# Layer 0's three products per weight tile: 272 + 272 + 272 columns become 288 + 256 + 272

## The chip, the core and the metric

One core of a Trainium2 chip runs the whole program. The time is the device time of one execution in microseconds (us), the median of several runs. The engines are named as in the profile: PE is TensorE (PEld its weight loads), DVE is VectorE, ACT is ScalarE, POOL is GpSimd, SP is SyncE, which here only issues loads.

## What is computed

A two-layer decoder trunk of width 2048 with 16 heads of 128, over 16 meta tokens and 256 tokens, 272 rows in all. Everything is float32:

```
h = concat([meta_tokens, x])                    # 272 x 2048
layer 0: a = rms_norm(h); q, k, v, f = split(a @ fox_w_in)
         o = forgetting_attention(q, k, v, cumsum(log_sigmoid(f + b)))
         h += o @ fox_w_o;   h += squared_relu_mlp(rms_norm(h), w_up[0], w_down[0])
layer 1: k, v = split(rms_norm(h) @ w_kv);  q = rms_norm(h) @ sb_w_q
         h += stick_breaking_attention(q, k, v) @ sb_w_o
         h += squared_relu_mlp(rms_norm(h), w_up[1], w_down[1])
return rms_norm(h)[16:]
```

Layer 0 needs all 272 rows, and so does the shared key and value projection `w_kv`. Behind the keys and values only the last 256 rows count, so layer 1's own products have 256 columns.

## The kernel before

The activations lie transposed: a feature is a partition, a token is a column, and 2048 features make 16 chunks of 128. Each weight matrix is cut into groups of 512 output features, `gemm_group` (L181) computes one group: 4 blocks `kb` of input features, each with 4 chunks `kc`, and 4 output tiles `m` of 128 features. Four PSUM accumulators `acc`, one bank for each `m`, hold the group's result. There are only these four buffers (L46), so a group's `m` can begin when the same `m` of the group before has been read out.

Each float32 factor is split into a rounded part `hi` and a remainder `lo` (type fp32r). A product of a weight tile (128 x 128) with a chunk is made of three matrix instructions: `whi` by the activations' `hi`, `whi` by their `lo`, `wlo` by their `hi` (L239 to L244). Each instruction has its own weight load. In the 272-column groups (`t0 == 0`, L241) the three follow each other for each tile; in the 256-column groups (L239) all tiles of a run come with one kind of product before the next kind.

The weights are streamed: SP issues loads of 512 KB into `raw` (4 buffers), ACT rounds a piece to `whi` (L222), DVE subtracts to get `wlo` (L223); 4 buffers of each hold two blocks `kb`. In the blocks 0 and 3 PE takes one `m` after the other through all four chunks (L233); in the blocks 1 and 2 it goes by half blocks (L235). So in the last block the accumulators end 12 instructions apart, and each `m` is needed again 36 instructions after its own end.

`evac` reads an accumulator out: into q, k, v (L356, L360), onto the residual stream (`residual_add`, L250), or through the squared ReLU (L486 to L490). In the output projections it is followed by the next split (L133, L134) and the sum of squares (L150, L151).

The split activations of one stage are in a tile of `xs` (class `Split`, L118): each chunk has 640 words; `ROWS` (L27) says where its `hi` and `lo` begin. For 272 columns `hi` begins at word 48 and `lo` at word 368, both at byte 192 of a 256-byte line; for 256 columns both begin at byte 0. The weights begin at byte 0 in the 272-column groups and at byte 64 in the others (L210 to L215).

The order of the matrix instructions of the groups is pinned (`gemm_matmul`, L173) but for the first group. All else on each engine is put in order by a scheduler, which goes by a timeline of its own, when the program is built.

Of the kernel before, what the change touches and what calls it, by code (L numbers as in the profile page):

```python
# [9 lines left out]
F32 = mybir.dt.float32  # L10
F32R = mybir.dt.float32r
AF = mybir.ActivationFunctionType
ALU = mybir.AluOpType
AX = mybir.AxisListType

P = 128
D = 2048
NC = D // P
M = 16
# [4 lines left out]
QSCALE = 1.0 / math.sqrt(P)  # L24
N_FF = 4

ROWS = {0: (48, 368), M: (0, 320)}  # L27
XROW = 640

G_A0, G_M0, G_KV, G_A1, G_M1, G_FIN = range(6)  # L30
# [3 lines left out]
def yoco_kernel(ctx: ExitStack, tc: tile.TileContext, hT_in, gains, b_f, w_f, w_qkv0, w_o0, w_up, w_dn,  # L34
                w_kv, w_q1, w_o1, outT):
    nc = tc.nc
# [7 lines left out]
    tmp = ctx.enter_context(tc.tile_pool(name="tmp", bufs=2))  # L44
# [73 lines left out]
    class Split:  # L118


        def __init__(self, label, t0):
            n = T - t0
            self.t0 = t0
            rows = xs.tile([P, NC * XROW + 64], F32R, tag="x", name=f"x_{label}")
            hi, lo = ROWS[t0]
            o = min(hi, lo)
            rows = rows[:, o:o + NC * XROW].rearrange("p (c t) -> p c t", c=NC)
            self.hi, self.lo = (rows[:, :, k - o:k - o + n] for k in (hi, lo))

    def split_chunk(sp, gi, c):  # L130

        g = g_sb[:, gi, c:c + 1]
        nc.scalar.activation(sp.hi[:, c], hT[:, c, sp.t0:], AF.Copy, scale=g)  # L133
        nc.vector.scalar_tensor_tensor(out=sp.lo[:, c], in0=hT[:, c, sp.t0:], scalar=g,  # L134
                                       in1=sp.hi[:, c].bitcast(F32), op0=ALU.mult, op1=ALU.subtract)
# [37 lines left out]
    def gemm_matmul(*args, **kw):  # L173

        ins = nc.tensor.matmul(*args, **kw).ins  # L175
        if queued and pinned[0]:
            tc.add_manual_dep(ins, queued[0].name, mybir.DependencyInfo(mybir.DependencyClass.NoSync,
                                                                        mybir.DependencyReason.DATA))
        queued[:] = [ins]

    def gemm_group(wblk, sp, t0, evac, before={}, after={}, load_x=None):  # L181

        uid[0] += 1
        u = uid[0]
        accs = [pacc.tile([P, 512], F32, tag="acc", name=f"acc_{u}_{m}") for m in range(4)]
        n = T - t0  # L190
        for kb in range(4):
            src_w = wblk[kb].rearrange("p (k c) -> p k c", k=4)
            if kb in before:
                before[kb]()
            piece = 1 if load_x is not None and kb < 2 else 2
            raws = [wraw.tile([P, 2, 512], F32, tag="raw", name=f"raw_{u}_{kb}_{hf}") for hf in range(2)]
            for k0 in range(0, 4, piece):
                if load_x is not None:
                    load_x(range(4 * kb + k0, 4 * kb + k0 + piece))
                if load_x is not None and kb == k0 == 0:  # L200

                    for c0 in (0, 256):
                        nc.scalar.dma_start(raws[0][:, 0, c0:c0 + 256], src_w[:, 0, c0:c0 + 256])
                else:
                    nc.sync.dma_start(raws[k0 // 2][:, k0 % 2:k0 % 2 + piece], src_w[:, k0:k0 + piece])
            parts = []
            for hf in range(2):
                whi = wspl.tile([P, 2 * 576], F32R, tag="whi", name=f"whi_{u}_{kb}_{hf}")
                wlo = wspl.tile([P, 2, 576], F32R, tag="wlo", name=f"wlo_{u}_{kb}_{hf}")
                if t0:  # L210
                    whi = whi.rearrange("p (k c) -> p k c", k=2)[:, :, 16:528]
                    wlo = wlo[:, :, 16:528]
                else:
                    whi = whi[:, :1024].rearrange("p (k c) -> p k c", k=2)
                    wlo = wlo[:, :, :512]  # L215
                boxes = [(o, piece, 0, 512) for o in range(0, 2, piece)]
                if load_x is not None and kb == hf == 0:
                    boxes[:1] = [(0, 1, 0, 256), (0, 1, 256, 512)]
                for o, no, c0, c1 in boxes:
                    src = raws[hf][:, o:o + no, c0:c1]  # L220
                    hp, lp = whi[:, o:o + no, c0:c1], wlo[:, o:o + no, c0:c1]
                    on_act = nc.scalar.activation(hp, src, AF.Copy)  # L222
                    on_dve = nc.vector.tensor_tensor(out=lp, in0=src, in1=hp.bitcast(F32), op=ALU.subtract)  # L223
                parts.append((whi, wlo))
            if kb in after:
                with tc.issue_after(on_act.ins), tc.issue_after(on_dve.ins):
                    after[kb]()


            if load_x is not None and kb == 0:  # L230
                runs = [([kc], range(4)) for kc in range(4)]
            elif kb in (0, 3):
                runs = [(range(4), [m]) for m in range(4)]  # L233
            else:
                runs = [(range(2 * hf, 2 * hf + 2), range(4)) for hf in range(2)]  # L235
            pinned[0] = load_x is None
            for kcs, ms in runs:
                if t0:
                    series = [(w, x, kc, m) for w, x in ((0, "hi"), (0, "lo"), (1, "hi")) for m in ms for kc in kcs]  # L239
                else:  # L240
                    series = [(w, x, kc, m) for m in ms for kc in kcs for w, x in ((0, "hi"), (0, "lo"), (1, "hi"))]  # L241
                for w, x, kc, m in series:
                    gemm_matmul(accs[m][:, :n], parts[kc // 2][w][:, kc % 2, m * P:(m + 1) * P],
                                getattr(sp, x)[:, 4 * kb + kc], start=kb == kc == w == 0 and x == "hi", stop=kb == kc == 3 and w == 1)  # L244
                if kb == 3:
                    for m in ms:
                        evac(m, accs[m][:, :n])

    def residual_add(c, acc, t0):
        nc.vector.tensor_tensor(out=hT[:, c, t0:], in0=acc, in1=hT[:, c, t0:], op=ALU.add)  # L250
# [6 lines left out]
    def load_x(chunks):  # L257
        c0, n = chunks[0], len(chunks)
        nc.sync.dma_start(hT[:, c0:c0 + n, :], hT_in[:, c0:c0 + n, :])
        if c0 == 0:  # L260
            nc.sync.dma_start(g_sb, gains)
        for c in chunks:
            split_chunk(xa, G_A0, c)
# [86 lines left out]
    for g in range(4):  # L350
# [11 lines left out]
        if g == 0:  # L362

            gemm_group(w_qkv0[0], xa, 0, lambda m, acc, qT=qT: nc.scalar.copy(qT[:, m, :], acc),
                       after={kb: (lambda kb=kb: first_norm(kb)) for kb in range(4)}, load_x=load_x)
            gate_products()
            box["rstd"] = norm.finish()
            for m in range(4):
                evac_q(m, qT[:, m, :])
            forget_gates(box["rstd"])  # L370
        else:
            gemm_group(w_qkv0[3 * g], xa, 0, evac_q)
# [4 lines left out]
        def decays(j):  # L377

            for i, (o, n) in enumerate(((0, 144), (144, T))):
                nc.vector.scalar_tensor_tensor(out=s[:, j, o:o + n], in0=fk[:, j, :n],  # L380
                                               scalar=fq_sb[:, i, 4 * g + j:4 * g + j + 1],
                                               in1=maskA[:, o:o + n], op0=ALU.subtract, op1=ALU.add)

        gemm_group(w_qkv0[3 * g + 1], xa, 0, lambda m, acc: evac_kv(m, acc, kT),
                   after={j: (lambda j=j: decays(j)) for j in range(4)})

# [31 lines left out]
        for pr in range(2):  # L418
            pp_sb = att.tile([P, 2, 416], F32, tag="pp", bufs=3, name=f"pp_sb_{g}_{pr}")
            for i in range(2):  # L420
# [14 lines left out]
                                in0=pm[:, P - M:P].unsqueeze(1).to_broadcast([P, 8, M]))  # L435
# [96 lines left out]
    for g in range(4):  # L532
# [30 lines left out]
        for pr in range(2):  # L563
# [3 lines left out]
            for i in range(2):  # L567
# [4 lines left out]
                                    in1=maskB[:, 0:256].unsqueeze(1).to_broadcast([P, 2, 256]))  # L572
            nc.vector.tensor_tensor(out=zp[:, :, 256:400], in0=pb[:, :, :144], op=ALU.add,
                                    in1=maskB[:, 256:400].unsqueeze(1).to_broadcast([P, 2, 144]))
            e = att.tile([P, 2, 416], F32, tag="pp", bufs=3, name=f"e_{g}_{pr}")[:, :, :400]
# [14 lines left out]
            for t in (240, 384):  # L590
                nc.vector.tensor_tensor(out=zp[:, :, t:t + M], in0=zp[:, :, t:t + M],
                                        in1=sc[:, 2 * pr:2 * pr + 2, :], op=ALU.add)
# [57 lines left out]
    for i in range(2):  # L650
        pr = patt.tile([P, 512], F32, tag="patt", name=f"pr_fin_{i}")
        for b in range(2):
            nc.tensor.matmul(pr[:, b * P:(b + 1) * P], rs[:, b:b + 1].to_broadcast([P, P]), ident,
                             start=True, stop=True)
# [4 lines left out]
    for c, n in [(12, 1), (13, 1), (14, 1), (15, 1), (0, 2), (2, 2), (4, 2), (6, 2)]:  # L659
        if n == 1:  # L660
            nc.vector.scalar_tensor_tensor(out=ob[:, c, :S], in0=hT[:, c, M:], scalar=g_sb[:, G_FIN, c:c + 1],
                                           in1=prs[0], op0=ALU.mult, op1=ALU.mult)
        else:
            nc.vector.tensor_tensor(out=ob[:, c:c + n, :S], in0=hT[:, c:c + n, M:], op=ALU.mult,  # L664
                                    in1=prs[0].unsqueeze(1).to_broadcast([P, n, S]))
        nc.sync.dma_start(outT[:, c:c + n, :], ob[:, c:c + n, :S])
    for c in (8, 10):
        nc.gpsimd.tensor_tensor(out=ob[:, c:c + 2, :S], in0=hT[:, c:c + 2, M:], op=ALU.mult,
                                in1=pr_sb.unsqueeze(1).to_broadcast([P, 2, S]))
# [52 lines left out]
```

## Time and profile before

| what | value |
|---|---|
| median of 3 runs | 2330.26 us (2329.82 to 2330.46) |
| the profiled execution's own time | 2329.83 us |
| its span, first to last instruction | 2328.0 us |
| granted PE clock | 0.998 |
| PE busy | 2316.8 us in 19030 instructions |
| DVE, ACT, POOL busy | 1289.9, 1040.6, 38.4 us |
| HBM read | 407.29 MB, 176 GB/s |

The span is 1.83 us shorter than the execution's own time, and that time is 0.43 us under the median. A PE instruction's recorded length overlaps with the next one's: what it costs is the distance from its start to the next start, which is got by dividing a stretch of the chain by the count of its instructions. The groups of 272 columns have 10752 matrix instructions, those of 256 columns 7680.

### The profile page before, as it was taken

How to read it: one execution, taken by the hardware profiler on the slowest of the kernel's cores; microseconds unless marked ns; L12 is line 12 of the kernel's file. 1: busy time of each engine (PE TensorE's matmuls, PEld its weight loads, DVE VectorE, ACT ScalarE, POOL GpSimd, SP SyncE). 2: the span in 40 equal slices, each digit the busy share in tenths (PEclk: the TensorE clock that was granted, in tenths of full speed). 3: DMA queues.
4: the chain of work that ended last, by engine and by line, in shares of the span. 5: the costliest groups of instructions: out<-in, count | busy, mean ns of one | idle time of the engine just before them, and what ended most of it. 6: DMA issues, size and time to landing. Idle time of an engine off the chain costs nothing.

```text
span 2328.0 us, 44800 instructions
## 1 busy us (share of the span) xinstructions
PE 2316.8 (100%) x19030; PEld 2309.8 (99%) x19030; DVE 1289.9 (55%) x1764; ACT 1040.6 (45%) x1397; POOL 38.4 (2%) x58
## 2 busy tenths in 40 slices
PE   9999999999999999999999999999999999999998
PEld 9999999999999999999999999999999999999998
DVE  7656556554455455455565555566555555555554
ACT  6444344443353344344544444455534434443553
POOL 1000000000000000000000000000000000000000
PEclk9999999999999999999999999999999999999999
DMA  7444545555555555555555444456565655656563
GB/s 240 166 163 157 181 154 168 185 174 180 181 170 185 172 184 177 183 170 184 173 188 183 156 153 149 152 180 199 180 192 178 194 182 184 195 182 191 179 192 127
DMA packets 116904, 412.32 MB, mean 177 GB/s; under 512 B 13520, under 2 KB 16992, under 8 KB 116704
## 3 DMA queue, kind: packets, MB, share of 16 engines
q1 hardware_dynamic: 114560, 406.29, 53.7%
q8 instruction: 149, 2.44, 0.4%
q10 hardware_dynamic: 2144, 3.17, 0.4%
q14 instruction: 51, 0.42, 0.1%
HBM read 407.29 MB, written 2.11 MB: 176 GB/s over the span
## 4 chain that ended last, share of the span: by engine, by line
PE 99%; DVE 0%; DMA 0%; ACT 0%; SPq 0%; issue 0%; DVEq 0%; ACTq 0%
PE acc L175 96%; PE ps L392 0%; PE pv L325 0%; PE pza L569 0%; PE po L454 0%; PE po L608 0%; DMA raw<-w_qkv 0%; PE po L609 0%; PE pzb L570 0%; PE po L455 0%; DVE ob L664 0%; PE pf L291 0%; PE pf L292 0%; PE pta L584 0%; PE pta L585 0%; PE pp L424 0%
## 5 line engine op out<-in xcount | busy, mean ns | idle before, releaser
L223 DVE TENSOR_TENSOR wlo<-raw,whi 128x1024 fp32r<-128x1024 f32 (+1 forms) x773 | 928.7, 1217 | 761.5 <-ACT whi L222 759.8
L222 ACT ACTIVATE whi<-raw 128x1024 fp32r<-128x1024 f32 (+1 forms) x773 | 796.5, 1049 | 1034.2 <-PE acc L175 1006.5
L175 PE MATMUL acc<-x_u,whi 128*128 128x272 f32 (+1 forms) x4096 | 651.9, 284 | 0.0
L175 PE MATMUL acc<-x_m,whi 128*128 128x272 f32 (+1 forms) x4096 | 651.7, 284 | 0.0
L175 PEld LDWEIGHTS acc<-x_u,whi 128*128 128x128 f32 x4096 | 573.9, 189 | 0.0
L175 PEld LDWEIGHTS acc<-x_m,whi 128*128 128x128 f32 x4096 | 573.6, 189 | 0.1
L175 PE MATMUL acc<-x_u,wlo 128*128 128x272 f32 (+1 forms) x2048 | 445.3, 284 | 0.0
L175 PE MATMUL acc<-x_m,wlo 128*128 128x272 f32 (+1 forms) x2048 | 445.2, 284 | 0.0
L175 PE MATMUL acc<-x_a,whi 128*128 128x272 f32 (+1 forms) x2048 | 361.8, 289 | 0.1
L175 PEld LDWEIGHTS acc<-x_u,wlo 128*128 128x128 f32 x2048 | 327.6, 189 | 0.0
L175 PEld LDWEIGHTS acc<-x_m,wlo 128*128 128x128 f32 x2048 | 327.5, 189 | 0.0
L175 PEld LDWEIGHTS acc<-x_a,whi 128*128 128x128 f32 x2048 | 303.4, 189 | 1.4 <-ACT whi L222 0.4
L175 PE MATMUL acc<-x_a,wlo 128*128 128x272 f32 (+1 forms) x1024 | 254.8, 287 | 0.0
L175 PE MATMUL acc<-x_kv,whi 128*128 128x272 f32 x1024 | 191.8, 288 | 0.0
L175 PEld LDWEIGHTS acc<-x_a,wlo 128*128 128x128 f32 x1024 | 176.5, 189 | 0.9 <-issue 0.5
L175 PE MATMUL acc<-x_o,whi 128*128 128x272 f32 (+1 forms) x1024 | 161.9, 282 | 0.0
L175 PEld LDWEIGHTS acc<-x_kv,whi 128*128 128x128 f32 x1024 | 159.7, 188 | 0.0
L175 PE MATMUL acc<-x_kv,wlo 128*128 128x272 f32 x512 | 147.5, 288 | 0.0
L175 PEld LDWEIGHTS acc<-x_o,whi 128*128 128x128 f32 x1024 | 141.7, 188 | 0.0
L250 DVE TENSOR_TENSOR hT<-acc,hT 128x272 f32<-128x272 f32 (+1 forms) x160 | 69.0, 431 | 88.1 <-PE acc L175 86.9
L175 PE MATMUL acc<-x_o,wlo 128*128 128x272 f32 (+1 forms) x512 | 110.5, 282 | 0.0
L175 PEld LDWEIGHTS acc<-x_kv,wlo 128*128 128x128 f32 x512 | 96.5, 188 | 0.0
(221 smaller groups left out, 969.2 us busy)
## 6 DMA issues: line engine op xcount, KB each, us to landing
raw<-w_up SPq DMA_DIRECT2D x256, 512.0 KB, 4.5
raw<-w_dn SPq DMA_DIRECT2D x256, 512.0 KB, 4.5
raw<-w_qkv SPq DMA_DIRECT2D x92, 512.0 KB, 3.8
raw<-w_o SPq DMA_DIRECT2D x64, 512.0 KB, 4.4
raw<-w_kv SPq DMA_DIRECT2D x64, 512.0 KB, 3.8
raw<-w_q SPq DMA_DIRECT2D x32, 512.0 KB, 4.5
fk<-f_dram ACTq DMA_DIRECT2D x4, 544.0 KB, 5.0
raw<-w_qkv SPq DMA_DIRECT2D x7, 256.0 KB, 4.5
```

The source lines that it names most:

```text
L175: ins = nc.tensor.matmul(*args, **kw).ins
L222: on_act = nc.scalar.activation(hp, src, AF.Copy)
L223: on_dve = nc.vector.tensor_tensor(out=lp, in0=src, in1=hp.bitcast(F32), op=ALU.subtract)
L250: nc.vector.tensor_tensor(out=hT[:, c, t0:], in0=acc, in1=hT[:, c, t0:], op=ALU.add)
```

## The change

In all groups with 272 columns the three products of a weight tile get other widths; their sum stays at 816 columns. `lo` now begins at word 320, right behind `hi`. A view `tail` reads the last 16 columns of `hi` and all 272 of `lo` as one run of 288 columns, beginning at byte 192 of a line as `hi` does. The products are now, in this order: `whi` by `tail` (288 columns, into columns 0 to 287 of the accumulator), `whi` by the first 256 columns of `hi` (into columns 16 to 271), `wlo` by all of `hi` (272 columns, into 16 to 287). So the first 16 columns of the accumulator hold the rounded product of the last 16 tokens, apart from the rest of their sum. When the group is done, ACT copies these 16 columns to a small tile `last`, DVE adds them onto columns 272 to 287 of the accumulator in place, and only then `evac` reads columns 16 to 287. The 256-column groups compute as before.

```diff
-ROWS = {0: (48, 368), M: (0, 320)}
+EXTRA = 16
+ROWS = {0: (48, 320), M: (0, 320)}
...
+            if not t0:
+                self.tail = rows[:, :, n - EXTRA:2 * n]
...
+                e = 0 if t0 else EXTRA
+                kinds = (0, "hi"), (0, "lo"), (1, "hi")
...
-                    series = [(w, x, kc, m) for m in ms for kc in kcs for w, x in ((0, "hi"), (0, "lo"), (1, "hi"))]
+                    series = [(w, x, kc, m) for m in ms for kc in kcs for w, x in (kinds[1], kinds[0], kinds[2])]
                 for w, x, kc, m in series:
-                    gemm_matmul(accs[m][:, :n], parts[kc // 2][w][:, kc % 2, m * P:(m + 1) * P],
-                                getattr(sp, x)[:, 4 * kb + kc], start=kb == kc == w == 0 and x == "hi", stop=kb == kc == 3 and w == 1)
+                    rhs, at = getattr(sp, x)[:, 4 * kb + kc], accs[m][:, e:e + n]
+                    if e and w == 0:
+                        rhs, at = ((sp.tail[:, 4 * kb + kc], accs[m][:, :e + n]) if x == "lo" else
+                                   (rhs[:, :n - e], accs[m][:, e:n]))
+                    gemm_matmul(at, parts[kc // 2][w][:, kc % 2, m * P:(m + 1) * P], rhs,
+                                start=kb == kc == w == 0 and x == ("lo" if e else "hi"), stop=kb == kc == 3 and w == 1)
                 if kb == 3:
                     for m in ms:
-                        evac(m, accs[m][:, :n])
+                        if e:
+                            last = tmp.tile([P, e], F32, tag="last", name=f"last_{u}_{m}")
+                            nc.scalar.copy(last, accs[m][:, :e])
+                            nc.vector.tensor_tensor(out=accs[m][:, n:n + e], in0=accs[m][:, n:n + e], in1=last, op=ALU.add)
+                        evac(m, accs[m][:, e:e + n])
```

More of the change, by code (lines that the diff above doesn't have):

```diff
@@ L237, in gemm_group @@
             for kcs, ms in runs:
+                e = 0 if t0 else EXTRA
+                kinds = (0, "hi"), (0, "lo"), (1, "hi")
                 if t0:
-                    series = [(w, x, kc, m) for w, x in ((0, "hi"), (0, "lo"), (1, "hi")) for m in ms for kc in kcs]
+                    series = [(w, x, kc, m) for w, x in kinds for m in ms for kc in kcs]
                 else:
-                    series = [(w, x, kc, m) for m in ms for kc in kcs for w, x in ((0, "hi"), (0, "lo"), (1, "hi"))]
+                    series = [(w, x, kc, m) for m in ms for kc in kcs for w, x in (kinds[1], kinds[0], kinds[2])]
                 for w, x, kc, m in series:
-                    gemm_matmul(accs[m][:, :n], parts[kc // 2][w][:, kc % 2, m * P:(m + 1) * P],
-                                getattr(sp, x)[:, 4 * kb + kc], start=kb == kc == w == 0 and x == "hi", stop=kb == kc == 3 and w == 1)
+                    rhs, at = getattr(sp, x)[:, 4 * kb + kc], accs[m][:, e:e + n]
[4 more added lines that the diff above has]
+                                start=kb == kc == w == 0 and x == ("lo" if e else "hi"), stop=kb == kc == 3 and w == 1)
                 if kb == 3:
                     for m in ms:
-                        evac(m, accs[m][:, :n])
+                        if e:
[3 more added lines that the diff above has]
+                        evac(m, accs[m][:, e:e + n])
     def residual_add(c, acc, t0):
```

## The prediction

> **What bounds the kernel now.** I read the page's busy times first, then its chain by engine, then the chain in order of time, then the PE groups with shapes kept apart.
>
> ```profile
> PE 2316.8 (100%) x19030; PEld 2309.8 (99%) x19030; DVE 1289.9 (55%) x1764; ACT 1040.6 (45%) x1397; POOL 38.4 (2%) x58
> PE 99%; DVE 0%; DMA 0%; ACT 0%; SPq 0%; issue 0%; DVEq 0%; ACTq 0%
> 439.91 756.83 PE acc L175 x6144
> 1602.36 708.08 PE acc L175 x6012
> 1512.87 89.07 PE acc L175 x785
> 78.29 13.56 PE acc L175 x107
> ```
>
> PE is busy throughout and is 99% of the chain that ended last; DVE and ACT work half the time. Only two things can move the time: the pace of PE's instructions, and a new wait of PE.
>
> The last four rows are pieces of the chain: start, length, count. Length by count is the distance from one start to the next. Layer 0's MLP, 272 columns wide: 756.83 / 6144 = 123.2 ns. Layer 1's MLP, 256 wide: 708.08 / 6012 = 117.8 ns. Layer 1's output projection, also 256 wide, same layout, same weights' place: 89.07 / 785 = 113.5 ns. A stretch of layer 0's attention, 272 wide: 13.56 / 107 = 126.7 ns. So **one width has two paces**, 3 to 4% apart, and each holds for a whole stage. Between the stages stands a norm's or an attention's matrix instruction; something about the phase of the stream locks in there. This is what the change plays with, and what the trace can't settle for new widths.
>
> **The change, part by part.** How many products it touches:
>
> ```profile
> L175 PE MATMUL acc<-x_m,whi 128*128 128x272 f32 x2048 | 379.3, 287 | 0.0
> L175 PE MATMUL acc<-x_u,whi 128*128 128x272 f32 x2048 | 379.0, 286 | 0.0
> L175 PE MATMUL acc<-x_a,whi 128*128 128x272 f32 x1536 | 293.7, 291 | 0.1
> L175 PE MATMUL acc<-x_kv,whi 128*128 128x272 f32 x1024 | 191.8, 288 | 0.0
> L175 PE MATMUL acc<-x_o,whi 128*128 128x272 f32 x512 | 95.1, 287 | 0.0
> ```
>
> Two instructions with `whi` per triple: (2048 + 2048 + 1536 + 1024 + 512) / 2 = 3584 triples. No instruction is added or taken away on PE, and the columns stay at 816 a triple. One nanosecond on a triple is 3.58 us of the kernel. (The 287 and 286 ns are recorded lengths that overlap; they are not the cost.)
>
> *Pace.* Now a triple takes 3 x 123.2 = 369.5 ns. Afterwards it is one instruction each of 288, 256 and 272. The trace has the last two widths, and one near relative of the first: fp32r products of 288 columns in layer 1's attention, as two runs of 144.
>
> ```profile
> 1503.59 0.39 PE L585 MATMUL pta<-el,ntri_r 128*128 128x512 f32 x1
> 1503.82 0.30 PE L586 MATMUL pta<-eh,nones_r 128*128 128x288 f32 x1
> 1503.95 0.30 PE L587 MATMUL pta<-el,nones_r 128*128 128x288 f32 x1
> 1504.08 0.29 PE L589 MATMUL ptb<-el,ntri_r 128*128 128x288 f32 x1
> 1504.21 0.40 PE L175 MATMUL acc<-x_o,whi 128*128 128x256 f32 x2
> ```
>
> Three 288s from 1503.82 to 1504.21: 390 / 3 = 130 ns each (the 512 before them 230 ns, which scaled to 288 is 129.4). Bounds:
>
> - 288 columns: below, 113.5 x 288 / 256 = 127.6 ns, the fast 256 pace scaled; above, 130 + (126.7 - 123.2) = 133.5 ns, the relative with the slow stretch's surcharge. I take 130, the nearest row.
> - 256 columns: 113.5 or 117.8 ns; I take 117.8, which held for 6012 instructions against 785.
> - 272 columns: 123.2 or 126.7 ns; I take 123.2, for the same reason.
>
> Sum taken: 130 + 117.8 + 123.2 = 371.0, which is 1.4 ns over 369.5 (unrounded rows), times 3584 = **+5 us**. All fast: 127.6 + 113.5 + 123.2 = 364.3, -5.2 ns, **-19 us**. All slow: 133.5 + 117.8 + 126.7 = 378.0, +8.5 ns, **+30 us**. That `lo` moves to another start within its chunk costs nothing I can see: nothing begins a PE read there any more, and all three reads keep byte 192 of a line.
>
> The Trainium skill has a rule here: "TensorE: Matmul & The Clock Gate", section "Back-to-back issue gap", gives the warm gap as columns / 2.4 plus 2.5 ns. By that, 272 columns would be 115.8 ns where this trace shows 123.2, so it does not price these instructions; being a straight line, it would leave the sum of the three widths as it is.
>
> *Reading out.* Each of the 56 x 4 = 224 accumulators gets an ACT copy of 16 columns and a DVE addition of 16 columns ahead of its `evac`. Neither size is in the trace. The nearest rows:
>
> ```profile
> L346 ACT ACTIVATE x_o<-pom 128x64 fp32r<-128x64 f32 x4 | 0.9, 223 | 1.7 <-PE pom L448 1.7
> L591 DVE TENSOR_TENSOR z<-z,sc 128x32 f32<-128x32 f32 x16 | 2.3, 183 | 0.0
> L134 DVE SCALAR_TENSOR_TENSOR x_m<-hT,g_sb,x_m 128x272 fp32r<-128x272 f32 x16 | 7.9, 495 | 0.2 <-ACT x_m L133 0.2
> L151 DVE TENSOR_TENSOR ssq_m<-ssq_m,sq_m 128x272 f32<-128x272 f32 x15 | 6.5, 434 | 0.0
> L490 DVE TENSOR_TENSOR x_u<-u,x_u 128x272 fp32r<-128x272 f32 x64 | 27.9, 436 | 1.7
> 616.69 2.01 ACT L222 ACTIVATE whi<-raw 128x1024 fp32r<-128x1024 f32 x2 [4.12 <-PE acc L175]
> 617.55 0.44 DVE L250 TENSOR_TENSOR hT<-acc,hT 128x272 f32<-128x272 f32 x1 [1.04 <-PE acc L175]
> 617.91 2.35 DVE L223 TENSOR_TENSOR wlo<-raw,whi 128x1024 fp32r<-128x1024 f32 x2
> ```
>
> As work, 224 x 0.22 = 49 us on ACT and 224 x 0.18 = 41 us on DVE disappear in engines that are half idle. As latency they matter: the accumulator is held longer. PE wants it again 36 instructions after its last product, 36 x 123.2 = 4.43 us.
>
> The built program's order on DVE puts the *fourth* accumulator's addition behind both `wlo` of the next group's block 1; before, its `evac` stood ahead of them. On ACT the fourth copy stands behind the two `whi`. From the last three rows: the fourth accumulator ends at about 617.5, the `wlo` pair at 617.91 + 2.35 = 620.26, 2.7 us later. The addition brings 2.9 and an `evac` of 0.44 brings 3.3 us: in the 25 groups with only this (the down projections but the last four, layer 0's values, the 8 groups of `w_kv`, the first group) and in the 16 up projections (one `x_u` remainder of 0.44 between, 3.8 us) 0.6 to 1.1 us of cover is left. The groups' own `whi` come when PE frees their buffers, so that isn't later than now.
>
> In 15 groups more stands between: the output projection and the last down projection (8 groups) have a split's remainder and a sum of squares behind the addition, 2.9 + 0.50 + 0.43 + 0.44 = 4.3 us, and their ACT halves (0.5 and 0.4 us) between the `whi`, so up to 5.2; seven query and key groups have DVE's softmax or decay work there, of like size. They are between 0 and 0.76 us late. I take 0.33 us, below the middle since part of those halves runs beside other waits: 15 x 0.33 = **+5 us**, bounds 0 and 15 x 0.76 = 11 us. What queues behind the late `evac` on DVE is the next `wlo`, which is two blocks ahead of PE.
>
> *Beginning.* The first product now needs the remainder of the first chunk.
>
> ```profile
> 4.96 0.50 DVE L134 SCALAR_TENSOR_TENSOR x_a<-hT,g_sb,x_a 128x272 fp32r<-128x272 f32 x1
> 6.58 0.41 PE L175 MATMUL acc<-x_a,wlo 128*128 128x272 f32 x2
> 7.14 1.27 PE L175 MATMUL acc<-x_a,whi 128*128 128x272 f32 x8
> ```
>
> It is there at 5.5 us; PE needs 12 x 0.123 = 1.5 us for the first chunk and waits until 7.14 for the second anyway. Cost nothing; without that cover, 0.5 us. The attention's own instructions move up to 24 places later in PE's order; they are the same instructions, so nothing.
>
> Sum, against the profiled execution's own 2329.83 us (span 2328.0): + 5 + 5 = **2340 us**. That is 0.4 us less than the same sum on the median of 2330.26.
>
> **The rivals.**
>
> *Fast (2306 to 2325, at the middle 2316).* Widths that are multiples of 32 settle into the fast pace. For it: the 785 instructions of 256 columns at 113.5 ns; and 272 costs 9.7 ns more than that for 16 columns, where 256 more columns (512 against 256) cost 116.5, 7.3 ns per 16. It has its place in the triples and decides from a triple below 368 ns (the waits' 5 us are 1.4 ns of it). Price -19 + 5 = -14 us; without waits and with 288 a little cheaper, -24. Against it: right after a norm the same 256 columns ran at 117.8 for 708 us.
>
> *Nothing (2330 to 2334).* The pace is a straight line through 256 at 117.8 and 272 at 123.2: 288 is 128.6, the triple is 369.5 as now, and the waits stay below 4.5 us. It is also what the cited page's line gives for the triples. Against it: the two paces per width lie on no line.
>
> *Slow lock (2352 to 2372).* Unequal widths keep the stream out of phase and the 126.7 ns pace becomes the rule: +30 us for pace, up to 11 for waits. For it: 107 instructions after a transpose; against it: 6144 in a row at 123.2.
>
> That the widths don't come out as described is no rival: PE's order in the built program has 288, 256, 272.
>
> **How the numbers follow.** Forecast, a triple of about 371 ns and some waits (2335 to 2350): 0.42. Fast 0.32, nothing 0.12, slow lock 0.14. A measurement of this kernel tells 0.2% (4.7 us) from no change: faster 0.32, same 0.12, slower 0.56. The range leaves out the fast case's last few us and the upper half of the slow lock: 2308 to 2360; the forecast's own is 2335 to 2350.
>
> **What would show it.** In the chain, layer 0's MLP as about 6144 instructions in 760 us, a triple at 371 ns; 364 or less means the fast case, 378 the slow lock. PE's idle time ended by DVE in the output projection and query groups, 0.3 us at a time, shows the waits; none there means I overrate them. The layer 1 stages, 113.5 and 117.8 ns, should stay; if one changes its pace there, its 4.3 ns on up to 6144 instructions (26 us) comes from a lock that I don't model, and would make the prediction wrong.

## The result, and the profile after

The changed kernel takes 2351.84 us (2351.30 to 2353.26, 4 runs) where the kernel before takes 2330.36 us (2329.82 to 2331.12, 4 runs) on the same chip: +21.5 us, a ratio of 1.0093 [1.0075, 1.0110]. The profiled execution's span is 2349.6 us against 2328.0, 21.6 us more. The change makes the kernel slower, as forecast, but by more than twice the 10 us that were forecast.

These are the page's busy times and its chain by engine, of the changed kernel:

```profile
PE 2330.3 (99%) x19030; PEld 2321.8 (99%) x19030; DVE 1326.8 (56%) x1988; ACT 1069.5 (46%) x1621; POOL 18.4 (1%) x58
PE 86%; DVE 1%; ACT 1%; issue 0%; DVEq 0%; ACTq 0%
```

As many PE instructions as before, 13.5 us more of busy PE; and DVE and ACT, which had no share of the chain that showed, now have 1% each. (PE's 86% against 99% is not a loss of that size: this chain could be followed back only to 285 us, and its shares are of the whole span.) So both of the forecast's costs came: pace and waits. The same chain in order of time (start, length, count; the first row is layer 0's MLP, the second layer 1's output projection, the last layer 1's MLP):

```profile
446.38 763.66 PE acc L179 x6144
1536.95 86.02 PE acc L179 x758
1623.40 708.08 PE acc L179 x6012
```

**Pace.** Layer 0's MLP went from 756.83 to 763.66 us with the same 6144 instructions: 124.3 ns each, 372.9 ns for a triple, 3.3 ns over the 369.5 of before. On 3584 triples that is 12 us. Layer 1's two stages keep 113.5 and 117.8 ns.

Such a piece of the chain goes from one norm's product to the next, and these stand some 100 products behind the start of their stage. So in both kernels 96 of the 6144 are 256-column products of layer 1. From the starts of layer 0's products alone, a triple takes 370.1 ns before and 373.4 after, made of 133.0 (288 columns), 116.25 (256) and 124.2 (272). The difference is the same 3.3 ns.

**Waits.** The rest lies in eight places where a PE instruction starts late, found as distances from start to start. Three are alike, in the query groups of layer 0. DVE's and PE's timeline of the changed kernel (start, length, instruction, idle time before and its releaser):

```profile
120.71 1.22 DVE L227 TENSOR_TENSOR wlo<-raw,whi 128x1024 fp32r<-128x1024 f32 x1
121.85 0.18 DVE L260 TENSOR_TENSOR acc<-acc,last 128x16 f32<-128x16 f32 x1
121.93 0.77 DVE L394 SCALAR_TENSOR_TENSOR s<-fk,fq_sb,maskA 128x144 f32<-128x144 f32 x2
122.62 0.43 DVE L370 SCALAR_TENSOR_TENSOR qT<-acc,rstd_a 128x272 f32<-128x272 f32 x1
```
```profile
122.55 0.28 PE L179 MATMUL acc<-x_a,wlo 128*128 128x272 f32 x1
123.20 0.37 PE L179 MATMUL acc<-x_a,whi 128*128 128x288 f32 x1 [0.37 <-DVE qT L370]
```

The addition stands behind a `wlo`, and two decay instructions (L394) stand between it and the `evac` that it serves. PE starts 0.65 us after its last start, 0.53 us more than the 0.12 of a product.

Four are in layer 1's value groups, and larger. The chain of the changed kernel there (start, length, what):

```profile
1341.24 0.28 ACT whi L226
...
1342.19 0.86 ACT e L555
1343.04 0.76 ACT z L609
1343.81 0.96 ACT whi L226
1344.79 1.23 DVE wlo L227
1346.11 0.89 DVE e L557
1346.99 0.35 DVE vT L374
1347.49 2.99 PE acc L179 x22
```

Read it backwards: PE waits for `vT`, the read-out of the fourth accumulator; on DVE that stands behind the softplus's last step `e` and behind `wlo`; `wlo` needs `whi`; and on ACT `whi` stands behind two exponentials of the attention. Only the addition (0.18 us at 1345.93, between `wlo` and `e`) is new work in it. What changed is the order. In the kernel before, DVE's timeline has the fourth `vT` ahead of both `wlo`:

```profile
1328.15 0.44 DVE L360 TENSOR_TENSOR vT<-acc,rstd_a 128x272 f32<-128x272 f32 x1 [0.71 <-PE acc L175]
1328.50 1.22 DVE L223 TENSOR_TENSOR wlo<-raw,whi 128x1024 fp32r<-128x1024 f32 x1
1329.64 1.08 DVE L580 TENSOR_TENSOR el<-e,eh 128x800 fp32r<-128x800 f32 x1
1330.64 1.21 DVE L223 TENSOR_TENSOR wlo<-raw,whi 128x1024 fp32r<-128x1024 f32 x1
```

The starts of PE are 1.44 us apart at 1346.05, 1404.78 and 1463.50, and 1.83 us at 1521.85: 3 x 1.31 + 1.70 = 5.6 us over a product's time. The eighth place is the first attention of layer 0, DVE's and PE's timeline:

```profile
65.56 1.22 DVE L227 TENSOR_TENSOR wlo<-raw,whi 128x1024 fp32r<-128x1024 f32 x1
66.69 0.17 DVE L260 TENSOR_TENSOR acc<-acc,last 128x16 f32<-128x16 f32 x1
...
67.44 0.42 DVE L374 TENSOR_TENSOR kT<-acc,rstd_a 128x272 f32<-128x272 f32 x1
```
```profile
65.89 0.28 PE L179 MATMUL acc<-x_a,wlo 128*128 128x272 f32 x1
67.91 0.97 PE L406 MATMUL ps<-kT,qT 128*128 128x144 f32 x4 [1.74 <-DVE kT L374]
```

Here PE waits not for an accumulator but for the keys themselves, 1.9 us over a product's time. (This one varies: 1.0 to 2.0 us from start to start in the runs that keep the read-out and the widths mixed.) Together 1.9 + 3 x 0.53 + 5.6 = 9.1 us. With 12 us of pace that is 21.1 of the 21.6 us by which the span is longer.

The read-out itself, from the groups by line (count, busy us and mean ns of one): the addition takes 179 ns where 180 were taken, the copy 166 where 220 were.

```profile
L260 DVE TENSOR_TENSOR acc<-acc,last 128x16 f32<-128x16 f32 x224 | 39.9, 179 | 49.4 <-ACT last L259 49.3
L259 ACT COPY last<-acc 128x16 f32<-128x16 f32 x224 | 37.1, 166 | 154.0 <-PE acc L179 148.1 <-DMA fqm_sb<-f_dram 5.8
```

### The profile page after: what moved, and what is told of

It is laid out like the page before. It is cut to its first block, busy times and chain, and to the rows that moved or that the text cites. A ratio compares the mean times of both kernels' runs of the same rounds, so it can differ in the third digit from the quotient of the medians.

```text
span 2349.6 us, 45417 instructions
## 1 busy us (share of the span) xinstructions
PE 2330.3 (99%) x19030; PEld 2321.8 (99%) x19030; DVE 1326.8 (56%) x1988; ACT 1069.5 (46%) x1621; POOL 18.4 (1%) x58
## 4 chain that ended last, share of the span: by engine, by line
PE 86%; DVE 1%; ACT 1%; issue 0%; DVEq 0%; ACTq 0%
PE acc L179 84%; PE pza L583 0%; PE po L622 0%; ACT whi L226 0%; DVE wlo L227 0%; PE pv L339 0%; PE po L623 0%; DVE e L557 0%; ACT e L555 0%; ACT z L609 0%; PE pzb L584 0%; PE ps L406 0%; DVE z L585 0%; DVE ob L678 0%; PE pta L598 0%
## 5 line engine op out<-in xcount | busy, mean ns | idle before, releaser
L179 PE MATMUL acc<-x_u,whi 128*128 128x256 f32 (+1 forms) x4096 | 655.3, 284 | 0.0
L179 PE MATMUL acc<-x_m,whi 128*128 128x256 f32 (+1 forms) x4096 | 655.1, 284 | 0.0
L179 PE MATMUL acc<-x_a,whi 128*128 128x256 f32 (+1 forms) x2048 | 359.5, 288 | 1.3 <-DVE qT L370 1.1
L179 PE MATMUL acc<-x_kv,whi 128*128 128x288 f32 (+1 forms) x1024 | 195.0, 289 | 3.5 <-DVE z L605 3.5
L179 PE MATMUL acc<-x_o,whi 128*128 128x256 f32 (+1 forms) x1024 | 162.9, 282 | 1.6 <-DVE z L605 1.6
L259 ACT COPY last<-acc 128x16 f32<-128x16 f32 x224 | 37.1, 166 | 154.0 <-PE acc L179 148.1
```

The costliest lines, as they stand in the source:

```text
L259: nc.scalar.copy(last, accs[m][:, :e])
```

## The experiments

Times are medians; "before" is the kernel before on the same chip in the same series, 2330.4 to 2330.9 us. The first two take the change apart.

**The widths without the read-out.** From the changed kernel:

```diff
-                            nc.scalar.copy(last, accs[m][:, :e])
-                            nc.vector.tensor_tensor(out=accs[m][:, n:n + e], in0=accs[m][:, n:n + e], in1=last, op=ALU.add)
```

> The changed kernel without the copy and the addition of the 16 columns (the rounded product of the last 16 tokens is left out of the result); PE's products as in the changed kernel. Theory A: of the 21 us lost, 12 are the pace of the three widths (layer 0's MLP 763.7 us against 756.8) and 9 are waits of PE for the fourth accumulator, which the two extra instructions put behind other work on VectorE. Then the time is about 2342 us, the MLP stays at 763.7 us and the gaps of 1.3 to 1.7 us at the values of layer 1 and of 0.5 us at the queries of layer 0 are gone. Rival B: the waits come from the new pace itself; then 2351 us, and the gaps stay.

2341.74 us (2340.94 to 2342.41), ratio 1.0045 [1.0030, 1.0060]. The chain's piece of layer 0's MLP:

```profile
443.23 763.54 PE acc L179 x6144
```

The MLP is as long as with the read-out, and none of the eight late starts is there. The widths alone cost about 11 us.

**The read-out without the widths.** The kernel before, its three products of 272 columns now into columns 16 to 287, with copy and addition:

```diff
-                    gemm_matmul(accs[m][:, :n], parts[kc // 2][w][:, kc % 2, m * P:(m + 1) * P],
...
+                    rhs, at = getattr(sp, x)[:, 4 * kb + kc], accs[m][:, e:e + n]
+                    gemm_matmul(at, parts[kc // 2][w][:, kc % 2, m * P:(m + 1) * P], rhs,
...
-                        evac(m, accs[m][:, :n])
+                        if e:
+                            last = tmp.tile([P, e], F32, tag="last", name=f"last_{u}_{m}")
+                            nc.scalar.copy(last, accs[m][:, e:2 * e])
+                            nc.vector.tensor_tensor(out=accs[m][:, n:n + e], in0=accs[m][:, n:n + e], in1=last, op=ALU.add)
+                        evac(m, accs[m][:, e:e + n])
```

> Three products of 272 columns as before, but each accumulator is read out as in the changed kernel: ACT copies 16 columns, VectorE adds them onto the last 16 (it adds the first 16 tokens' sums onto the last 16's, so the result differs). Theory A: 2330.4 + 9 = about 2339 us, layer 0's MLP at 756.8 us as before, and the same gaps as in the changed kernel. Rival B: no gaps, 2330 us.

2341.45 us (2340.07 to 2342.57), ratio 1.0044 [1.0029, 1.0059]:

```profile
443.45 756.93 PE acc L176 x6144
```

The MLP is that of before. The late starts are there at the same eight places: 1.93 us in the first attention, three of 0.70, three of 1.51, one of 1.85 from start to start. The waits alone cost about 11 us, and 11 + 11 is the change's 21.5: the two parts add up and don't hide one another.

**The order within a triple.** 256, 288, 272 instead of 288, 256, 272, but for the first tile of an accumulator:

```diff
-                    series = [... for w, x in (kinds[1], kinds[0], kinds[2])]
+                    series = [... for w, x in ((kinds[1], kinds[0], kinds[2]) if kb == kc == 0 else kinds)]
```

> The changed kernel with the order 256, 288, 272 within each triple but an accumulator's first. Theory of widths: each width has its price wherever it stands, layer 0's MLP stays at 763.7 us within 0.5 and the whole at 2351.8. Rival, neighbours: the price of an instruction hangs on the one before it; then the MLP moves by more than 2 us, the sign isn't foreseen.

2353.78 us (2352.97 to 2353.98), ratio 1.0097 [1.0081, 1.0112]:

```profile
447.40 764.89 PE acc L179 x6144
```

1.2 us longer than with the change's order, a triple of 373.5 instead of 372.9 ns. That lies between what the two theories allowed and decides for neither. From start to start, in triples of the new order that follow one another, the single products moved more than their sum: 288 columns 133.0 to 131.5, 256 columns 116.25 to 118.2, 272 columns 124.2 to 123.9 ns. A product's price depends on what stands beside it.

**One width alone: three of 288, and three of 256.** In the changed kernel:

```diff
-                    if e and w == 0:
-                        rhs, at = (...)
+                    if e:
+                        rhs, at = sp.tail[:, 4 * kb + kc], accs[m][:, :e + n]
```

> All three products of a layer-0 weight tile are 288 columns wide and take the low part's last 16 columns with the high part, so the operands of the first and third product are not the right ones; readout as in the changed kernel. Theory A (a product has a price by its width, whatever stands beside it): the 288-column product keeps the 132.9 ns that it took in the changed kernel, so the chain's piece of 6144 products of layer 0's MLP lasts 6144 x 132.9 = 816.5 us, and the kernel about 2330.4 + 10752 x (132.9 - 123.2) ns + 9.5 us of waits = 2444 us. Theory B (what was predicted, 130 ns, is the price of the width, and the excess comes from changing width inside a triple): 6144 x 130.0 = 798.7 us, kernel about 2413 us.

```diff
+                    if e:
+                        first = kb == kc == w == 0 and x == "lo"
+                        rhs, at = ((sp.tail[:, 4 * kb + kc], accs[m][:, :e + n]) if first else
+                                   (rhs[:, :n - e], accs[m][:, e:n]))
+                        if x == "lo" and not first:
+                            rhs = sp.tail[:, 4 * kb + kc, :n - e]
```

> All products of layer 0 are 256 columns wide but the first one of each accumulator (which clears all 288 columns); the last 16 tokens get next to nothing of their products. All begin at the place that the changed kernel uses. Theory A (price by width): 116.3 ns as measured for the 256-column product inside the changed kernel's triples, MLP of layer 0 6144 x 116.3 = 714.5 us, kernel about 2330.4 - 10752 x (123.2 - 116.3) ns + 9.5 = 2266 us. Theory B (a stream of one width locks at one of layer 1's two paces): 113.35 ns (696.4 us; kernel 2234) or 117.8 ns (723.8 us; kernel 2282). With the run of three 288s: if (288) + (256) + 123.2 comes to 372.9 the triple is the sum of its widths' uniform prices; if it comes to less, changing the width costs by itself.

One run each, 2437.81 and 2248.75 us. Layer 0's MLP with 288 columns, and with 256:

```profile
471.77 817.66 PE acc L179 x6144
```
```profile
421.19 702.64 PE acc L179 x6144
```

288 columns: 817.66 / 6144 = 133.1 ns, as theory A had it; not 130. 256 columns: 114.4 ns; with the 128 first products of 288 taken out at 133.1, (702.64 - 128 x 0.1331) / 6016 = 114.0 ns, nearer to layer 1's 113.35 than to 117.8 or to the 116.3 beside other widths. So theory A holds for 288 and not for 256. The 130 of the prediction is in the run of three 288s too: 3024 of its 6046 starts of 288 columns stand 130 ns apart, the others 136 or 137. The sum by which the two runs were to be read: 133.1 + 114.0 + 123.2 = 370.3 ns. The mixed triple takes 372.9. By this sum, 0.7 of the 3.3 ns that the change adds come from the widths themselves and 2.6 from their standing side by side. The split hangs on the price of 256 columns, which has two paces in this kernel: with 117.8 the parts would come to 374.1, more than the mixture. So the two runs alone don't show that mixing costs.

**The widths in runs, and the control.** If a change of width costs, it should be enough to have fewer of them. The changed kernel, with the three kinds one after another for each run of four or eight tiles:

```diff
-                    series = [(w, x, kc, m) for m in ms for kc in kcs for w, x in (kinds[1], kinds[0], kinds[2])]
+                    series = [(w, x, kc, m) for w, x in (kinds[1], kinds[0], kinds[2]) for m in ms for kc in kcs]
```

> The changed kernel with layer 0's products in another order: for each run of four or eight weight tiles all 288-column products, then all 256, then all 272, so that the width changes 0.75 or 0.38 times per triple instead of 3 times; the same result. The uniform streams took 133.1 ns (288), 114.0 ns (256, with the 128 first products at 133.1 taken out) and 123.2 ns (272), 370.3 ns together, where the mixed triple takes 372.9. Theory A (a change of width costs about 0.9 ns by itself): 370.3 + 0.5 = 370.8 ns, layer 0's MLP 759 us instead of 763.7 and the kernel about 7 us less, 2345 us. Theory B (the mixed triple's 372.9 has another cause, such as where its weights and operands lie): 763.7 us and 2352 us.

The control is the kernel before with the same order:

> The control for the run before: the kernel before, three products of 272 columns, in that order of runs. Theory A (only changes of width cost): layer 0's MLP 756.9 us as it was, kernel 2330 us within 2. Theory B (the order itself moves the pace, by the weights that follow one another): the MLP moves by the same 4 to 5 us as the changed kernel's.

Control: 2330.67 us (2329.67 to 2331.94), ratio 1.0000 [0.9991, 1.0010]. Widths in runs: 2350.1 us (2346.12 to 2352.96), ratio 1.0089 [1.0072, 1.0106], not to be told from the change by its time. Layer 0's MLP in the control, and with the widths in runs:

```profile
440.38 756.83 PE acc L175 x6144
```
```profile
449.56 753.65 PE acc L179 x6084
```

The order alone moves nothing. With three widths it does. The piece is 60 products shorter and holds only 36 of layer 1's 256-column products, so its 123.9 ns can't be set beside the 124.3 above; from the starts of layer 0's products alone a triple takes 371.8 ns instead of 373.4. Theory A has the right sign and not its whole size: 1.6 ns went, where it expected 2.1. About 1 ns over the sum of the uniform streams stays when runs are four to eight products long; why, is open. On 3584 triples 1.6 ns are 5.7 us, and the span of the one profiled execution, the fastest at 2346.12 us, is 5.2 us shorter than the changed kernel's. Its late starts moved but add up to about as much as before: in the query groups, where both `wlo` now stand ahead of the read-out, three grew from 0.65 to between 1.62 and 1.82 us; those of the value groups are gone, and one of 1.5 us came ahead of layer 1's output projection. The other three executions took 2349.56 to 2352.96 us and left no profile, so why they are longer is open.

**The value groups not read out.** To see whether the waits sit where the chain puts them, the changed kernel without copy and addition in layer 1's four value groups:

```diff
-    def gemm_group(wblk, sp, t0, evac, before={}, after={}, load_x=None):
+    def gemm_group(wblk, sp, t0, evac, before={}, after={}, load_x=None, read=True):
...
-                        if e:
+                        if e and read:
...
-        gemm_group(w_kv[2 * g + 1], xc, 0, lambda m, acc: evac_kv(m, acc, vT))
+        gemm_group(w_kv[2 * g + 1], xc, 0, lambda m, acc: evac_kv(m, acc, vT), read=False)
```

> The changed kernel without the copy and the add in the four value groups of layer 1 (w_kv's odd blocks), 16 of the 224 accumulators: their last 16 tokens lose the first product. Theory A (the new waits stand where VectorE's row puts wlo and e ahead of the fourth accumulator's release; four of them are in these groups, 1.44, 1.44, 1.44 and 1.83 us from start to start): the four waits go, 2351.8 - 5.7 = 2346 us, and the 0.65 us waits of the query groups and the 2.02 us of the first attention stay. Theory B (every read-out delays its release by its own two instructions, and the 9 to 11 us lie evenly on the 224 accumulators): 10 x 16/224 = 0.7 us less, 2351 us.

2348.68 us (2347.59 to 2348.92), ratio 1.0077 [1.0063, 1.0091]: between the two numbers. The trace says why. All four late starts of the value groups are gone, and the three of 0.65 us and the one in the first attention (1.71 us here) are left, as theory A has it. But the chain of this run has, for layer 1's output projection and the MLP behind it:

```profile
1535.09 85.78 PE acc L179 x727
...
1621.30 708.08 PE acc L179 x6012
```

85.78 / 727 = 118.0 ns, where the changed kernel has 86.02 / 758 = 113.5. That stage fell into the other of its two paces: 727 x 4.5 ns = 3.3 us given back, and 5.6 - 3.3 = 2.3 is near the 2.6 us by which the span is shorter. The products began at 113 ns and went over to 117.8 at 1536.5, where two starts are 220 ns apart. The run of three 256s has the same: 220 ns between two starts at 1435.4, and from there on the slow pace, again 727 products in 85.78 us. That the small stop is the cause isn't shown: in the run with widths in runs the same stage has a late start of 1.5 us at 1535.3 and goes on at 81.21 / 714 = 113.7 ns.

**The two paces of layer 1.** The prediction found one width at two paces and could not say what chooses. In the kernel before, the pace of 117.8 ns begins at the norm's product of 256 columns (`pms_m`, L156), and the one of 113.5 follows attention products of which the last is 32 columns wide. The change of pace can be seen inside one stage, PE's timeline of the kernel before:

```profile
1599.05 1.98 PE L175 MATMUL acc<-x_m,whi 128*128 128x256 f32 x16
1600.86 1.07 PE L175 MATMUL acc<-x_m,wlo 128*128 128x256 f32 x8
1601.77 0.59 PE L156 MATMUL pms_m<-ssq_m,mean_w 128*128 128x256 f32 x2
...
1605.03 2.05 PE L175 MATMUL acc<-x_m,whi 128*128 128x256 f32 x16
1606.91 1.10 PE L175 MATMUL acc<-x_m,wlo 128*128 128x256 f32 x8
```

Sixteen products of the same MLP take 1.81 us from start to start ahead of the norm's product (113 ns each) and 1.88 us behind it (117.5). So the pace does not belong to the stage. The next run is the kernel before, with the norm's product cut in two, the last 32 columns by themselves:

```diff
-            nc.tensor.matmul(ps[:, :n], mean_w, self.acc[:, self.t0:], start=True, stop=True)
+            for c0, c1 in ((0, n - 32), (n - 32, n)):
+                nc.tensor.matmul(ps[:, c0:c1], mean_w, self.acc[:, self.t0 + c0:self.t0 + c1], start=True, stop=True)
```

> The kernel before, with each norm's matrix product over the tokens (one instruction of 272 or 256 columns) cut into two, the last of 32 columns; same result. Theory of the lock: the instruction just ahead of a stream of equal products sets which of its two paces it keeps; a narrow one sets the fast pace. Then layer 1's MLP goes from 117.8 to 113.5 ns, from 708 to 682 us, the queries of layer 1 gain 3 us, and the whole is about 2301 us; layer 0's MLP may move either way. Rival: the pace belongs to the stage (its tiles, its data); then nothing moves, 2330 us.

2301.24 us (2300.78 to 2301.99), ratio 0.9873 [0.9856, 0.9889]: faster than both kernels. The chain at layer 1's first products and at its MLP, each piece behind its norm:

```profile
1197.02 0.55 PE pms_a L157 x4
1197.57 103.64 PE acc L176 x894
...
1599.41 0.52 PE pms_m L157 x4
1599.93 681.46 PE acc L176 x6012
```

The MLP runs at 681.46 / 6012 = 113.35 ns behind its norm; the norm costs 0.1 us more. The same edit on the changed kernel:

> The changed kernel, with the norm's product cut into two (all but the last 32 columns, then the last 32), which took the kernel before from 2330.9 to 2301.2 us. Theory A (the short product just ahead of a stream sets that stream's pace where there are two paces to choose from, in layer 1's 256-column streams alone): 2351.8 - 29.7 = 2322 us, layer 1's MLP 681.5 us instead of 708.1, layer 0's 763.7 as it was. Theory B (the changed kernel's triples too have two paces, and 372.9 ns is the slow one): layer 0's MLP shorter as well, by up to 3.8% (4.45 of 117.8 ns), 735 us, and the kernel about 2293 us. Theory C (the gain belongs to the order of work in the kernel before): 2352 us.

2323.06 us (2322.37 to 2324.04), ratio to the kernel before 0.9969 [0.9957, 0.9981]:

```profile
446.02 763.74 PE acc L180 x6144
...
1620.44 681.46 PE acc L180 x6012
```

Theory A: layer 1 gains the same 26.6 us in its MLP, and layer 0's mixed triples keep their 372.9 ns. They have no second pace that this edit reaches. With the norm in two in both kernels, the change still costs 2323.06 - 2301.24 = 21.8 us.

Last, a short product in the middle of a stream, the kernel before with:

```diff
             u = Split(f"u{layer}_{f}", t0)
+            if (layer, f) == (1, 2):
+                short = patt.tile([P, 512], F32, tag="patt", name="short")
+                gemm_matmul(short[:, :32], mean_w, mean_w[:, :32], start=True, stop=True)
```

> The kernel before with one product of 32 columns (into an accumulator that nobody reads) ahead of the third quarter of layer 1's MLP, held at its place in TensorE's order; the same result. Theory A (a stream of 256-column products keeps the pace at which it began until something comes between, and a short product ahead of it makes it begin at 113.35 ns): the second half of the MLP, 3072 products, runs at 113.35 instead of 117.8 ns, 13.7 us less, 2317 us. Theory B (only the stop at the norm, where the stream begins after a wait, lets it choose): 2330.5 us, all at 117.8. Theory C (a stream that is interrupted falls to the slow pace, as 0.1 us of wait did in the output projection of the run with unread values): 2330.5 us too, the same as B; told apart from A alone.

2316.65 us (2316.31 to 2317.78), ratio 0.9942 [0.9927, 0.9957]. The chain's two halves of the MLP, the second beginning behind the short product:

```profile
1601.69 350.51 PE acc L175 x2976
...
1952.34 344.18 PE acc L175 x3036
```

117.8 ns in the first half, 344.18 / 3036 = 113.4 in the second: theory A to the microsecond. No stop and no norm is needed; one product of 32 columns between two products of 256 moves the whole stream behind it. What these runs don't separate is the width of 32 from a mere count: that each product put between changes the pace over fits them too, since one does so here and at the norm of the kernel before, and the norm in two leaves the pace as it was. No run puts a product of another width at this place.

## Why the prediction was right and wrong

- **What bounds the kernel** was right: nothing but PE's pace and new waits of PE moved the time, and the two parts, run alone, add up to the whole.
- **Pace: this step failed.** It made the triple as the sum of three prices, each from a stream of its own, 130 + 117.8 + 123.2 = 371.0 ns, and +5 us. In the changed kernel the three products take 133.0 + 116.25 + 124.2 = 373.4 ns, 3.3 more than before, +12 us. The term that was furthest off is the price of 288 columns: 130 ns came from three products in the attention, and in a long stream only half of the starts are 130 apart; the mean is 133.1, near the upper bound of 133.5. Taking 117.8 for 256 columns was too dear, here and in the run of three 256s (114.0), and made up for half of that, which was luck. The other thing that failed is the adding. A width's price is not its own: it moves by up to 2 ns with its neighbours, and the same three widths, grouped by width, take 1.6 ns less. How much the mixture costs over its parts stays open, since 256 columns have two prices.
- **Two readings of the lines were wrong.** "Each holds for a whole stage" isn't so: layer 1's MLP begins at 113 ns and changes over at its norm's product. And the 6144 products of "layer 0's MLP" include 96 of 256 columns; 272 columns alone take 123.4 ns, not 123.2. Neither decides the outcome.
- **Waits: this term was too small as well, and its places were wrong.** 15 groups at 0.33 us were to give 5 us, with a bound of 11; it was 9.1 us in eight places. Of the 15 named groups only the three query groups hold up an accumulator, by 0.53 us each. The four largest are value groups, which stood in the list with "0.6 to 1.1 us of cover". That list took the time from accumulator's end to `wlo` pair from an MLP group, where ACT has nothing between the two `whi`; in the value groups ACT has two exponentials (0.86 and 0.76 us on the chain) there and DVE has `e` (0.89 us) behind the addition. The eighth, 1.9 us in the first attention, is of a kind that the step did not consider: PE needing the read-out's result, not its buffer.
- **Beginning**: nothing was to be paid there, and nothing is shown to have been. In PE's timeline of the changed kernel the eight products that waited for the second chunk at 7.14 us begin at 7.27.

```profile
7.27 1.26 PE L179 MATMUL acc<-x_a,whi 128*128 128x288 f32 x8
```

In two runs whose first product doesn't need the remainder, the products behind this wait begin at 7.11 (the read-out without the widths) and 7.29 us (the short product midway), so 0.13 us is within what runs differ by.

- **The rivals.** *Fast* rested on multiples of 32 settling into a faster pace: 256 columns alone do (114.0 ns), 288 don't (133.1), and mixed they don't; the norm in two, which gives layer 1 its fast pace, leaves the triples alone. *Slow lock* wanted a triple of 378 ns; it was 372.9. The time came close to its lower end by another way. *Nothing* had both wrong: the triple went up by 3.3 ns, and the waits are 9.1 us, not below 4.5.
- **Layer 1's stages** stayed at their paces in the changed kernel, as the forecast needed. The caveat that a stage may change its pace was right: in the run with unread values it took back over half of the gain.

## What to carry to other kernels

Price a stream of matrix instructions as the mixture that will run, not as the sum of a few rows from elsewhere: here three products in the attention gave 130 ns for a width that takes 133 in a long stream, and the same widths cost 1.6 ns per triple less when grouped. When a read-out gets one more small instruction, look at the order that the scheduler then writes on each engine: 0.18 us of addition let the read-out slip behind a `wlo` that waits on ACT's exponentials, and cost 1.3 us at a time. And where one width shows two paces, look at the instruction ahead of the stream: here cutting the norms' products in two was worth 29.7 us, more than the change under study costs.

## What the runs showed of the hardware that was not expected

A stream of 256-column fp32r products runs at 117.8 ns (6012 products in 708.08 us) behind a float32 product of 256 columns, and at 113.35 ns (681.46 us) behind one of 32 columns, and mostly holds the pace for thousands of products; a 32-column product in the middle moves it from 117.8 to 113.4. A 256-column norm's product does the opposite inside a stage: 113 ns ahead of it, 117.5 behind. The pace can also fall back without a product between, as at 1536.5 us in the run with unread values and at 1435.4 in that of three 256s, each time at a stop of about 0.1 us; what makes it fall is open. Layer 0's streams of 272 columns (756.83 us before, 756.91 with the norm in two) and of three widths (763.66 and 763.74) did not react. In a triple of 288, 256 and 272 columns the price of one width moved by up to 2 ns with the order of the three, and the sum by only 0.6. A stream of 288 columns has no single gap: 130 ns at half of its starts, 136 or 137 at the others.
